# The last layer's down projection of a two-layer decoder trunk, written as seven block products instead of eight

## The chip, the cores and the metric

The kernel runs on one core of a Trainium2 chip, as one program and one launch. The metric is device time in microseconds (us). The core has five engines that work side by side, each through its own stream of instructions in a fixed order: TensorE (PE in the profile; its weight loads are PEld), VectorE (DVE), ScalarE (ACT), GpSimd (POOL) and SyncE (SP), which here only issues DMAs. Where an instruction needs another engine's result it waits for a semaphore, and everything behind it in its own stream waits too.

## The reference

Two layers, each a token mixer with three branches and then a gated MLP with a short causal convolution, and a final RMSNorm. There are 512 tokens of width 1024, in float32. Only the end of the second layer is touched by the change:

```python
def conv_ffn(h, w_up, conv_w, conv_b, w_down):
    u = h @ w_up
    ...
    gate, val = jnp.split(c, 2, axis=-1)
    return (jax.nn.silu(gate) * val) @ w_down

x = x + conv_ffn(rmsnorm(x, norm2_g[l]), ffn_w_up[l], ffn_conv_w[l], ffn_conv_b[l], ffn_w_down[l])
...
return rmsnorm(x, final_g)
```

The product with w_down has 512 rows (tokens), an inner dimension of 2816 (22 blocks of 128) and 1024 columns. The activation silu(gate) * val comes out with the inner dimension on the partitions, 128x512 for each of the 22 blocks.

## The kernel before

Matrices are multiplied in float32 by splitting each operand into a rounded high part and the rest. ACT casts the high part (line 135 for weights, 1066 for activations), DVE subtracts it from the original for the low part (136, 1067), and `mm3` (line 152) issues three matmuls: high x low, high x high, low x high. A matmul has a 128x128 block as its stationary operand and 128x512 as its moving one.

`ffn_up` runs the up projection for i = 0 to 21. For each i it makes two columns of blocks (gate and value), scales them (1054), convolves (1056 to 1058), applies the gate (1062 to 1064) and splits the result into the pair `act[i]`. For odd i under 17 it also turns one block of the residual x into rows, over DRAM with POOL's DMA queue (`turned`, 226 and 230), into `xt`.

`last` is the down projection of the second layer and the end of the program. The stationary operand is a block of an activation (128 tokens), the moving one a weight tile (128x512). First all four row blocks c of the left half of the columns: for k in 22, one weight unit and 4 x 3 matmuls into four PSUM tiles of the pool `acc`. Then the right half, into four PSUM tiles of the pool `sm`: 16 units in the same way, and the last 6 (`KEPT`) are kept in memory, so that row blocks finish one after another and the scaling and output of a row block run beside the products of the next. The left half's sums are read from PSUM, added to x (1106), squared (1109) and multiplied by the final gain on POOL (1123) while the right half is multiplied. The row's scale comes from a root on ACT (1137) and a reciprocal on DVE (1138); ACT scales the left half (1149), DVE the right one (1151), and ACT's and SP's queues write them out.

Weight units are loaded by SP and split a few units ahead (`unit`, `load`, `part`). The order of instructions on each engine is set when the program is built, by a scheduler that works from the program's order with its own estimates; instructions under `keep_in_program_order` (`po`, and every matmul while `self.pin` is set) stay as written.

Of the kernel before, what the change touches and what calls it, by code (L numbers as in the profile page):

```python
# [48 lines left out]
class Emit:  # L49
# [95 lines left out]
        self.nc.vector.tensor_tensor(lo, src, hi, op=SUB)  # L145
        return hi, lo

    def mm3(self, ps, w, x, start, stop):
        (wh, wl), (xh, xl) = w, x

        def mm(*x, **y):
            i = self.nc.tensor.matmul(*x, **y)  # L152
# [881 lines left out]
    def ffn_up(self, l, st, x):  # L1034
        nc, V, A = self.nc, self.nc.vector, self.nc.scalar
        nt = [0]
        self.xt = []

        def at():
            nt[0] += 1  # L1040
            return (self.f if nt[0] <= NFP else self.r)(dt=F32R, n="ah")

        act = []
        first = self.firstF(l, (78, 79, 80), st, (3,))
        for i in range(NFF):
            if x and i % 2 == 1 and i < 17:
                o = self.r(n="xt")
                self.turned(o, self.r(n="xT"), x[i // 2], nc.gpsimd)
                self.xt.append(o.rearrange("p (a c d) -> p c a d", c=4, d=32))
            cs = []  # L1050
            for j in (i, NFF + i):
                ps = first.pop(0) if first else self.colF(l, 78 + 2 * i + (j >= NFF))
                u = self.u(n="fu")
                V.tensor_tensor(u, ps, self.rsF, op=MUL)  # L1054
                t = self.u(n="cv")
                A.activation(t, u, AF.Identity, scale=self.p("cw2", j), bias=self.p("cb", j))  # L1056
# [7 lines left out]
            V.tensor_tensor(th, th, v, op=MUL)  # L1064
# [22 lines left out]
    def last(self, act):  # L1087


        nc, V, A, P, po = self.nc, self.nc.vector, self.nc.scalar, self.nc.gpsimd, self.tc.keep_in_program_order  # L1090
        fg = [self.u(n="fg") for _ in range(2)]
        for h in range(2):
            nc.sync.dma_start(fg[h], self.a["fgr"][:, 512 * h:512 * h + 512].to_broadcast([128, 512]))
        ss, bias = self.small((128, NC), "fss", 1), self.small((128, NC), "fbi", 1)
        self.pin = True

        def prod(ps, k, c, w):
            cs = slice(128 * c, 128 * c + 128)
            ah, al = act[k]
            self.mm3(ps, (ah[:, cs], al[:, cs]), w, k == 0, k == NFF - 1)  # L1100

        def add(y, ps, j, c):

            b = slice(j % 4 * 128, j % 4 * 128 + 128)
            q = lambda t: t[:, b].rearrange("p (a d) -> p a d", d=32)
            return V.scalar_tensor_tensor(q(y), q(ps), 0.5, self.xt[j][:, c], op0=MUL, op1=ADD)

        def square(y, s):
            return A.activation(self.u(n="sq")[:, 0:y.shape[1]], y, AF.Square, accum_out=s)

        self.pool = None
        pss = [self.acc() for _ in range(NC)]
        for k in range(NFF):
            w = self.unit("wdt", 0, k, 0)
            for c in range(NC):
                prod(pss[c], k, c, w)
        ya = []
        for c in range(NC):
            y = self.u(n="ya")
            for j in range(4):  # L1120
                add(y, pss[c], j, c)
            square(y, ss[:, c:c + 1])
            P.tensor_tensor(y, y, fg[0], op=MUL)
            ya.append(y)
        V.tensor_scalar(bias, ss, 1.0 / D, 1e-6, op0=MUL, op1=ADD)
        pss = [self.sm() for _ in range(NC)]
        for k in range(NFF - KEPT):
            w = self.unit("wdt", 0, k, 512)
            for c in range(NC):
                prod(pss[c], k, c, w)  # L1130
        self.pool = "u"
        ws = [self.unit("wdt", 0, k, 512) for k in range(NFF - KEPT, NFF)]

        def factor(s, b):

# [2 lines left out]
            po(V.reciprocal(rs, rs))  # L1138
            return rs

        for c in range(NC - 1):
            for k, w in enumerate(ws, NFF - KEPT):
                prod(pss[c], k, c, w)
            y, s = self.u(n="yb"), self.small((128, 1), "fs1")
            for j in range(4, 8):
                po(add(y, pss[c], j, c))
            po(square(y, s))
            rs = factor(s, bias[:, c:c + 1])
            po(A.activation(ya[c], ya[c], AF.Copy, scale=rs))
            nc.scalar.dma_start(self.a["out"][c, :, 0:512], ya[c])  # L1150
            po(V.scalar_tensor_tensor(y, y, rs, fg[1], op0=MUL, op1=MUL))
            nc.sync.dma_start(self.a["out"][c, :, 512:1024], y)
        c, y, b = NC - 1, self.u(n="yb"), bias[:, NC - 1:]
        for k, w in enumerate(ws, NFF - KEPT):
            prod(pss[c], k, c, w)
        for j in range(4, 8):
            po(add(y, pss[c], j, c))
        s = [self.small((128, 1), f"fs{i}", 1) for i in (2, 3)]
        for i in range(2):
            po(square(y[:, 256 * i:256 * i + 256], s[i]))  # L1160
        po(V.scalar_tensor_tensor(b, s[0], 1.0 / D, b, op0=MUL, op1=ADD))
        rs = factor(s[1], b)
        for i in range(2):
            h = slice(256 * i, 256 * i + 256)
            po(V.scalar_tensor_tensor(y[:, h], y[:, h], rs, fg[1][:, h], op0=MUL, op1=MUL))
            nc.sync.dma_start(self.a["out"][c, :, 512 + 256 * i:768 + 256 * i], y[:, h])
            po(A.activation(ya[c][:, h], ya[c][:, h], AF.Copy, scale=rs))
            nc.scalar.dma_start(self.a["out"][c, :, 256 * i:256 * i + 256], ya[c][:, h])

# [111 lines left out]
```

## Time and profile before

| | |
|---|---|
| Time of three runs | 1712.87, 1715.34, 1715.23; median 1715.23 us |
| Span of the profiled execution | 1712.1 us |
| Down projection of the last layer, left half | 1585.8 to 1645.7 us |
| Right half | 1645.8 to 1705.65 us |
| Rest after the last matmul | 1705.65 to 1712.1 us |

The profiled execution is another one than the three timed; its own time is the span from the first instruction to the last. Rows of instruction groups give line, engine, operation, output and inputs by the program's names, shapes, the count, and the busy time with the mean of one in ns; then the engine's idle time before them and who ended it. Rows of a timeline give start and duration in us. Rows of a tile's view give the shortest, median and longest duration in ns, and the first and last start in us. Rows of windows give the stretch, its length, busy time and count of PE, PEld, DVE, ACT and POOL, the granted clock of TensorE, the share of DMA and GB/s.

### The profile page before, as it was taken

The page shows a single profiled execution, that of the slowest core. Times are in us where ns is not written, and L with a number is a line of the kernel's source. Part 1 is how long each engine was busy: PE and PEld are TensorE (multiplying, and loading weights), DVE is VectorE, ACT ScalarE, POOL GpSimd, SP SyncE. Part 2 cuts the span into 40 slices and gives each one's busy share as a digit, 9 for nine tenths or more (in the row PEclk, how much of TensorE's full clock was granted, in tenths as well). Part 3 has the DMA queues.
Part 4 walks back from the last instruction along what each step waited for, and adds up shares of the span by engine and source line. Part 5 has one row for each costly group of instructions (what it writes and reads, how often), then busy time and mean ns, then how long its engine had stood idle before and what let it go on. Part 6 is the DMA issues. An engine that isn't in the chain of part 4 may idle for free.

```text
span 1712.1 us, 27377 instructions
## 1 busy us (share of the span) xinstructions
PE 1701.0 (99%) x10280; PEld 1392.4 (81%) x10280; DVE 1155.0 (67%) x1998; ACT 774.9 (45%) x1315; POOL 178.2 (10%) x213
## 2 busy tenths in 40 slices
PE   9999999999999999999999999999999999999998
PEld 7888777788888888888888888777888888888886
DVE  6887745578669777753368887555776787787333
ACT  6563443554255444433355634345533554444223
POOL 2121000003200000000021210100141011100010
PEclk9999999999999999999999999999999999999999
DMA  5236553525542333233432365535254433333333
GB/s 180 87 109 205 174 174 99 178 89 163 163 148 93 98 99 96 69 113 114 123 105 87 107 222 168 159 122 178 77 185 147 137 122 117 113 109 99 99 99 105
DMA packets 132325, 219.61 MB, mean 128 GB/s; under 512 B 16864, under 2 KB 37088, under 8 KB 132192
## 3 DMA queue, kind: packets, MB, share of 16 engines
q1 hardware_dynamic: 116336, 180.94, 34.4%
q0 software_dynamic: 6784, 20.98, 3.8%
q10 hardware_dynamic: 9072, 15.94, 2.6%
q8 instruction: 81, 1.33, 0.3%
q14 instruction: 52, 0.43, 0.1%
HBM read 188.43 MB, written 29.36 MB: 127 GB/s over the span
## 4 chain that ended last, share of the span: by engine, by line
PE 89%; DMA 5%; DVE 3%; ACT 1%; issue 1%; SPq 1%; ACTq 0%; POOL 0%; DVEq 0%; POOLq 0%
PE acc L152 80%; PE sm L152 4%; PE sm L640 2%; DMA wr<-wall 2%; PE sm L893 1%; DVE wl L136 1%; PE sm L547 1%; DMA ws<-sgw 1%; DMA tr<-yt 0%; DMA tr<-bkT 0%; SPq L226 0%; DMA bkS<-tr 0%; PE sm L998 0%; DMA x<-xT 0%; DMA tr<-qkt 0%
## 5 line engine op out<-in xcount | busy, mean ns | idle before, releaser
L152 PE MATMUL acc<-hi,sh 128*128 128x512 f32 x1108 | 431.9, 390 | 0.0
L152 PE MATMUL acc<-lo,sh 128*128 128x512 f32 x1108 | 431.6, 390 | 0.0
L152 PE MATMUL acc<-hi,sl 128*128 128x512 f32 x1108 | 430.6, 390 | 0.0
L135 ACT CAST sh<-wr 128x512 fp32r<-128x512 f32 (+1 forms) x347 | 212.2, 615 | 356.6 <-PE acc L152 264.3
L136 DVE TENSOR_TENSOR sl<-wr,sh 128x512 fp32r<-128x512 f32 (+1 forms) x347 | 236.1, 683 | 139.9 <-ACT sh L135 74.9
L136 DVE TENSOR_TENSOR wl<-wr,wh 128x512 fp32r<-128x512 f32 x233 | 165.2, 710 | 184.9 <-ACT wh L135 182.3
L135 ACT CAST wh<-wr 128x512 fp32r<-128x512 f32 x233 | 144.1, 619 | 281.1 <-PE acc L152 182.3
L152 PEld LDWEIGHTS acc<-hi,sl 128*128 128x128 f32 x1108 | 208.0, 188 | 43.7 <-DVE gth L1013 0.3
L152 PEld LDWEIGHTS acc<-lo,sh 128*128 128x128 f32 x1108 | 208.0, 188 | 43.6 <-issue 0.9
L152 PEld LDWEIGHTS acc<-hi,sh 128*128 128x128 f32 x1108 | 208.0, 188 | 43.6 <-issue 0.3
L152 PE MATMUL acc<-lo,wh 128*128 128x512 f32 x588 | 232.5, 395 | 0.5 <-DVE lo L211 0.3
L152 PE MATMUL acc<-hi,wl 128*128 128x512 f32 x588 | 230.3, 392 | 0.5 <-DVE wl L136 0.5
L152 PE MATMUL acc<-hi,wh 128*128 128x512 f32 x588 | 229.5, 390 | 0.0
L152 PEld LDWEIGHTS acc<-lo,wh 128*128 128x128 f32 x588 | 110.5, 188 | 26.3 <-DVE lo L211 1.6
L152 PEld LDWEIGHTS acc<-hi,wl 128*128 128x128 f32 x588 | 110.5, 188 | 25.9 <-DVE wl L136 2.3
L152 PEld LDWEIGHTS acc<-hi,wh 128*128 128x128 f32 x588 | 110.6, 188 | 22.4 <-issue 0.2
L152 PE MATMUL acc<-ah,sh 128*128 128x512 f32 x352 | 108.4, 389 | 0.0
L1054 DVE TENSOR_TENSOR fu<-acc,rsF 128x512 f32<-128x512 f32 x88 | 60.6, 688 | 56.4 <-PE acc L152 56.3
L1056 ACT ACTIVATE cv<-fu,pc 128x512 f32<-128x512 f32 x88 | 71.6, 816 | 46.7 <-DVE fu L1054 44.4
L1057 DVE SCALAR_TENSOR_TENSOR cv<-fu,pc,cv 128x511 f32<-128x511 f32 x88 | 65.8, 748 | 21.1 <-ACT cv L1056 20.6
L152 PE MATMUL acc<-wl,hi 128*128 128x512 f32 x192 | 78.3, 408 | 0.0
L152 PEld LDWEIGHTS acc<-ah,sh 128*128 128x128 f32 x352 | 66.1, 188 | 13.7
(312 smaller groups left out, 2345.4 us busy)
## 6 DMA issues: line engine op xcount, KB each, us to landing
wr<-wall SPq DMA_DIRECT2D x488, 256.0 KB, 2.7
gd<-gth ACTq DMA_DIRECT2D x48, 256.0 KB, 3.0
gth<-gd POOLq DMA_DIRECT2D x48, 256.0 KB, 3.6
wr<-wdt SPq DMA_DIRECT2D x44, 256.0 KB, 2.6
wr<-wdn SPq DMA_DIRECT2D x40, 256.0 KB, 2.7
tr<-bkT SPq DMA_DIRECT2D x16, 256.0 KB, 2.8
bkS<-tr SPq DMA_DIRECT2D x128, 32.0 KB, 2.5
tr<-vT SPq DMA_DIRECT2D x8, 256.0 KB, 2.6
```

Of the source, the lines that this page charges most:

```text
L135: self.kept(self.nc.scalar.copy(hi[:, :n], raw[:, :n]))
L136: self.kept(self.nc.vector.tensor_tensor(lo[:, :n], raw[:, :n], hi[:, :n], op=SUB))
L152: i = self.nc.tensor.matmul(*x, **y)
L547: i = T.matmul(pK[hv[1 - h], j, :], bk[hv[h], c, 1, :], x[hv[h], c, :], start=True, stop=True)
L640: po(T.matmul(o, l, r, start=start, stop=True, skip_group_check=True))
L893: po(T.matmul(X[h][:, i, :], lhsT, rhs, start=new[h], stop=stop, skip_group_check=True))
L1054: V.tensor_tensor(u, ps, self.rsF, op=MUL)
L1056: A.activation(t, u, AF.Identity, scale=self.p("cw2", j), bias=self.p("cb", j))
L1057: V.scalar_tensor_tensor(t[:, 1:], u[:, :511], self.p("cw1", j), t[:, 1:], op0=MUL, op1=ADD)
```

## The change

The product is divided into 2 x 2 x 2 blocks: rows (tokens 0 to 255, 256 to 511), inner dimension (even and odd blocks of 128, so a pair q = 0 to 10 is blocks 2q and 2q+1) and columns (left, right). Instead of eight block products, seven are made, with sums of halved blocks on both sides. They are numbered 1 to 7 in the code. Products 7, 5, 6 and 4 use sums of weight blocks; products 1, 2 and 3 use weight blocks as they are. Products 1, 2 and 4, 3 use activations as they are or one sum of all four.

In `ffn_up` of the last layer, `halves` takes the two activations a and b of a pair and makes, on POOL, s (two sums of 256 tokens), d and the difference that replaces the left of b; s and b are split for group 1. The unsummed halves (`ab`) and d (two pairs to a tile, `s4`) go to DRAM by POOL's DMA queue.

In `last`, group 1 runs over q: `sums(q)` loads four weight blocks and makes four sums of them, three on POOL and one on DVE; `ring` splits each of them (ACT and DVE). `sums(q + 1)` is written ahead of the products of q. After a pair's products its `ab` tile is loaded again and split. Group 2 runs product 1 over all q, then 3 and 2 over the first six pairs, then 2 and 3 over the five kept ones row block by row block. The four PSUM results of a row block are combined into v1, v2 and v3 between the groups, and x is added on POOL (`addx`, four pieces of 128 columns). Rows 2 and 3 are finished after product 1; rows 0 and 1 at the end. `KEPT` goes from 6 to 5.

```diff
-KEPT = 6
+KEPT = 5
...
-    def mm3(self, ps, w, x, start, stop):
+    def mm3(self, ps, w, x, start, stop, **kw):
...
-            hi, lo = at(), at()
-            A.copy(hi, th)
-            V.tensor_tensor(lo, th, hi, op=SUB)
-            act.append((hi, lo))
+            if l < L - 1:
+                act.append(self.split(th, at))
+            elif i % 2 == 0:
+                even = th
+            else:
+                act.append(self.halves(even, th, i // 2, at))
         return act
+
+    def halves(self, a, b, q, at):
+        P, h = self.nc.gpsimd, [slice(0, 256), slice(256, 512)]
+        s, d = [self.wp.tile([128, 512], F32, name=self.nm(t), tag=t, bufs=3) for t in ("wh", "wl")]
+        P.tensor_tensor(s[:, h[0]], a[:, h[1]], b[:, h[1]], op=ADD)
+        P.tensor_tensor(s[:, h[1]], s[:, h[0]], a[:, h[0]], op=SUB)
+        P.tensor_tensor(d[:, h[0]], b[:, h[0]], s[:, h[1]], op=SUB)
+        ab = self.dp.tile([128, 512], F32, name=self.nm("ab"))
+        if q % 2 == 0:
+            self.s4 = self.dp.tile([128, 512], F32, name=self.nm("s4"))
+        for o, i in ((ab[:, h[0]], a[:, h[0]]), (ab[:, h[1]], b[:, h[0]]), (self.s4[:, h[q % 2]], d[:, h[0]])):
+            P.dma_start(o, i)
+        P.tensor_tensor(b[:, h[0]], a[:, h[0]], a[:, h[1]], op=SUB)
+        return self.split(s, at), self.split(b, at), ab, self.s4
...
+        Q, H = NFF // 2, [slice(0, 512), slice(512, 1024)]
+        def ring(w):
+            nring[0] += 1
+            if nring[0] % 2:
+                hi, lo = [self.wp.tile([128, 512], F32R, name=self.nm(t), tag=t, bufs=3) for t in ("wh", "wl")]
+            else:
+                hi, lo = [self.u(dt=F32R, n=t) for t in ("sh", "sl")]
+            A.copy(hi, w)
+            V.tensor_tensor(lo, w, hi, op=SUB)
+            return hi, lo
...
+        def sums(q):
+            b12, b22, b11, b21 = [raw(2 * q + j, n) for j, n in ((0, 1), (1, 1), (0, 0), (1, 0))]
+            P.tensor_tensor(b22, b22, b12, op=SUB)
+            P.tensor_tensor(b12, b12, b11, op=SUB)
+            V.tensor_tensor(b11, b11, b22, op=ADD)
+            P.tensor_tensor(b21, b21, b11, op=SUB)
+            return [ring(w) for w in (b22, b12, b11, b21)]
...
+        pss = {p: [(self.acc if p in (7, 5) else self.sm)() for _ in range(2)] for p in (7, 5, 6, 4)}
+        W, ab = [sums(0)], []
...
+        for q in range(Q):
+            if q + 1 < Q:
+                W.append(sums(q + 1))
+            s, t = act[q][:2]
+            w = dict(zip((7, 5, 6, 4), W.pop(0)))
+            for p in (7, 5, 6, 4) if q < Q - 1 else (6, 7, 5, 4):
+                x, at = {7: (t, 0), 5: (s, 0), 6: (s, 256), 4: (t, 256)}[p]
+                for r in range(2):
+                    prod(pss[p][r], x, at, r, w[p], q == 0, q == Q - 1)
+            o = self.u(n="ab")
+            nc.sync.dma_start(o, act[q][2])
+            ab.append(self.split(o, self.f))
...
+        seq = [(1, q) for q in range(Q)]
+        k0 = Q - KEPT
+        for g in range(0, k0, 3):
+            seq += [(p, q) for p in (3, 2) for q in range(g, min(g + 3, k0))]
+        kept = [(p, q) for p in (2, 3) for q in range(k0, Q)]
...
+        def addx(y, h, c):
+            for j in range(4):
+                b = y[:, 128 * j:128 * j + 128].rearrange("p (a d) -> p a d", d=32)
+                P.tensor_tensor(b, b, self.xt[4 * h + j][:, c], op=ADD)
+        def plus(y, ps, z, rows=slice(0, 512)):
+            return V.scalar_tensor_tensor(y[:, rows], ps[:, rows], 0.5, z[:, rows], op0=MUL, op1=ADD)
...
+        ahead(3)
+        for r in range(2):
+            e, f, g = [self.f(n=t) for t in ("v1", "v2", "v3")]
+            A.activation(e, pss[6][r], AF.Copy, scale=0.5)
+            plus(f, pss[7][r], e)
+            plus(g, pss[5][r], e)
+            plus(e, pss[4][r], f)
+            plus(f, pss[5][r], f)
+            addx(e, 0, 2 + r)
+            addx(f, 1, 2 + r)
+            addx(g, 1, r)
...
+        for p, q in seq:
+            ahead(1)
+            for r in range(2):
+                go(p, q, r, units[p, q])
+            if (p, q) != (1, Q - 1):
+                continue
+            for r in range(2):
+                plus(v3[r], one[r], v3[r])
+                plus(v1[r], one[r], v1[r])
+                plus(v2[r], one[r], v2[r])
+            for r in range(2):
+                c, (ya, yb) = 2 + r, (v1[r], v2[r])
+                s1, b = self.small((128, 1), "fs1"), ss[:, c:c + 1]
+                square(ya, b)
+                square(yb, s1)
+                V.tensor_scalar(b, b, 1.0 / D, 1e-6, op0=MUL, op1=ADD)
+                rs = self.small((128, 1), "frs", 4)
+                A.activation(rs, s1, AF.Sqrt, scale=1.0 / D, bias=b)
+                V.reciprocal(rs, rs)
+                P.tensor_tensor(ya, ya, fg[0], op=MUL)
+                A.activation(ya, ya, AF.Copy, scale=rs)
+                nc.gpsimd.dma_start(self.a["out"][c, :, 0:512], ya)
+                V.scalar_tensor_tensor(yb, yb, rs, fg[1], op0=MUL, op1=MUL)
+                nc.gpsimd.dma_start(self.a["out"][c, :, 512:1024], yb)
...
+        ahead(len(kept))
+        for r in range(2):
+            for p, q in kept:
+                go(p, q, r, units[p, q])
...
```

`ahead(n)` loads and splits the next n weight tiles of group 2 (through `ring`, or into kept tiles), `go` issues the three matmuls of one weight tile and one block of 128 rows, and `raw` is a load of one 128x512 weight tile by SP.

More of the change, by code (lines that the diff above doesn't have):

```diff
@@ L1037, in ffn_up, with at @@
         self.xt = []
-        def at():
+        def at(**kw):
             nt[0] += 1
@@ new lines, in last, with ahead @@
+        kept = [(p, q) for p in (2, 3) for q in range(k0, Q)]
+        units, todo = {}, iter(seq + kept)
+        def ahead(n):
+            for _, (p, q) in zip(range(n), todo):
+                w = raw(2 * q + (p > 1), p == 3)
+                if (p, q) in kept:
+                    hi, lo = [self.u(dt=F32R, n=t) for t in ("sh", "sl")]
+                    A.copy(hi, w)
+                    V.tensor_tensor(lo, w, hi, op=SUB)
+                    units[p, q] = hi, lo
+                else:
+                    units[p, q] = ring(w)
@@ L1125, in last @@
[L1125 to L1132, printed above, removed]
         def factor(s, b):
@@ L1139, in factor @@
             return rs
[L1141 to L1168, printed above, removed]
+        ahead(3)
@@ new lines, in last @@
+        v1, v2, v3 = [], [], []
+        for r in range(2):
[8 more added lines that the diff above has]
+            addx(g, 1, r)
+            v1.append(e), v2.append(f), v3.append(g)
+        one = [self.sm() for _ in range(2)]
@@ new lines, in last @@
+        out = {1: one, 2: one, 3: [self.acc() for _ in range(2)]}
+        for p, q in seq:
[22 more added lines that the diff above has]
+                nc.gpsimd.dma_start(self.a["out"][c, :, 512:1024], yb)
```

82 lines of the change are left out of this document (56 added, 26 removed).

## The prediction, made before the run

> **What bounds the kernel now.** I read the page's busy times and chain first, then the down projection of the last layer by its tiles, then its two stretches.
>
> ```profile
> span 1712.1 us, 27377 instructions
> PE 1701.0 (99%) x10280; PEld 1392.4 (81%) x10280; DVE 1155.0 (67%) x1998; ACT 774.9 (45%) x1315; POOL 178.2 (10%) x213
> PE 89%; DMA 5%; DVE 3%; ACT 1%; issue 1%; SPq 1%; ACTq 0%; POOL 0%; DVEq 0%; POOLq 0%
> ...
> L152 PE MATMUL acc<-wh,ah x176: 389/389/389, 1586.0 to 1645.4; 128*128 128x512 f32 x176
> ...
> L152 PE MATMUL sm<-wh,ah x128: 389/389/389, 1645.9 to 1688.9; 128*128 128x512 f32 x128
> ...
> L152 PE MATMUL acc<-wl,ah x88: 389/389/389, 1585.8 to 1645.0; 128*128 128x512 f32 x88
> ...
> L152 PE MATMUL sm<-wl,ah x64: 389/389/389, 1645.6 to 1688.5; 128*128 128x512 f32 x64
> ...
> L152 PE MATMUL sm<-sh,ah x48: 388/389/389, 1689.4 to 1705.3; 128*128 128x512 f32 x48
> ...
> L152 PE MATMUL sm<-sl,ah x24: 389/389/389, 1689.2 to 1704.8; 128*128 128x512 f32 x24
> ...
> 1645.80 59.85 PE sm L152 x264
> 1705.65 0.02 issue
> ...
> 1585.60:1645.40 59.80, 59.80 (x265) 49.53 (x264) 19.27 (x32) 15.13 (x25) 0.00 (x0) 1.00 0.30 96
> 1645.40:1705.70 60.30, 60.24 (x266) 49.55 (x264) 23.89 (x52) 21.36 (x41) 5.95 (x4) 1.00 0.31 98
> ```
>
> TensorE is the bound of the whole program and more so here: 176 + 128 + 88 + 64 + 48 + 24 = 528 matmuls run from 1585.8 to 1705.65 without a break. A record lasts 389 ns but matmuls overlap; the chain row gives the price on the path, 59.85 / 264 = 0.2267 us. In the same two stretches DVE is busy for 43 of 120 us, ACT for 36, POOL for 6, and DMA 0.3 of its capacity. All those helpers are hidden behind TensorE; after the last matmul there are 6.45 us of row scaling and output.
>
> **What is removed.** Seven products of eight leave 7 x 11 x 2 x 3 = 462 matmuls: 66 x 0.2267 = **-15.0 us**, the whole possible gain, if TensorE still never waits. The rest of this part asks where it waits.
>
> **Group 1 and the lock between DVE and POOL.** Per pair q of inner blocks, TensorE has 4 products x 2 x 3 = 24 matmuls, 5.44 us. The new helpers for one q: POOL subtracts three times 128x512, DVE adds once and splits five times (four weight sums, one reloaded ab tile), ACT casts five times, SP loads five tiles of 256 KB. Counted apart they fit, with durations from the rows here and below: POOL 3 x 1.29 = 3.9, DVE 6 x 0.68 = 4.1, ACT 5 x 0.62 = 3.1; DMA moves 1.31 MB, 241 GB/s, by the row above (0.31 at 98) a share of 0.76. But the only POOL tensor operations in the old down projection show that they cannot be counted apart:
>
> ```profile
> 1646.13 1.29 POOL L1123 TENSOR_TENSOR ya<-ya,fg 128x512 f32<-128x512 f32 x1 [132.26 <-ACT sq L1109]
> 1646.79 1.18 DVE L136 TENSOR_TENSOR wl<-wr,wh 128x512 fp32r<-128x512 f32 x1
> 1647.38 1.74 POOL L1123 TENSOR_TENSOR ya<-ya,fg 128x512 f32<-128x512 f32 x1
> ...
> 1649.08 1.29 POOL L1123 TENSOR_TENSOR ya<-ya,fg 128x512 f32<-128x512 f32 x1
> ...
> 1649.26 1.66 DVE L136 TENSOR_TENSOR wl<-wr,wh 128x512 fp32r<-128x512 f32 x1 [0.50 <-ACT wh L135]
> ...
> 1650.33 1.74 POOL L1123 TENSOR_TENSOR ya<-ya,fg 128x512 f32<-128x512 f32 x1
> 1652.01 0.68 DVE L136 TENSOR_TENSOR wl<-wr,wh 128x512 fp32r<-128x512 f32 x1
> ```
>
> A DVE split that meets no POOL operation takes 0.68 (last row). The two that start inside one end 0.55 after it: 1647.97 against 1647.42, and 1650.92 against 1650.37. The POOL operations that start inside such a split end 1.15 after it: 1649.12 and 1652.07. They take turns, whole instruction by whole instruction, with 1.15 for POOL and 0.55 for DVE. So one q needs 3 x 1.15 + 6 x 0.55 = 6.75 us of turns, more than TensorE's 5.44, and group 1 is bound by the turns: 11 x 6.75 - 11 x 5.44 = **+14.4 us**. Below: no waiting for turns, where POOL's own loop (two subtractions, DVE's add, the third: 2 x 1.25 + 0.1 + 0.69 + 1.29 = 4.6) stays under 5.44, so 0. Above: turns of full length, 3 x 1.29 + 6 x 0.68 = 7.95, so 11 x 2.51 = 27.6. I take the measured turns.
>
> [...]
>
> **Start of group 1.** Before, k = 0 needs only old activations, so TensorE goes straight on while the last one is finished:
>
> ```profile
> 1585.57 0.39 PE L152 MATMUL acc<-hi,sl 128*128 128x512 f32 x1
> 1585.80 0.39 PE L152 MATMUL acc<-wl,ah 128*128 128x512 f32 x1
> ...
> 1586.00 0.69 DVE L1054 TENSOR_TENSOR fu<-acc,rsF 128x512 f32<-128x512 f32 x1 [1.22 <-PE acc L152]
> ...
> 1589.51 0.68 DVE L136 TENSOR_TENSOR wl<-wr,wh 128x512 fp32r<-128x512 f32 x1
> 1590.11 0.68 DVE L1064 TENSOR_TENSOR fth<-fth,cv 128x512 f32<-128x512 f32 x1
> ...
> L226 POOL DMA_DIRECT2D xt<-tr x32 | 17.4, 551 | 20.1 <-PE acc L152 9.2 <-ACT sh L135 6.0 <-ACT cv L1056 2.6
> ```
>
> In the changed program's order, POOL's stream has the first subtraction of sums(0), then the first operation of halves for the last pair, then a DMA issue, and only then the second subtraction of sums(0). That halves operation waits for the last activation, which ends at 1590.79, 4.8 us after the last up-projection matmul (4.2 without the weight split that then stood between). Behind it: POOL 0.75 (128x256, half of 1.29 and some start; bounds 0.65, and 0.96 with the 0.31 of POOL's smallest copy, below) + 0.55 + 1.29 = 2.6. DVE's stream then has the add, the split of b12 and only third the split of b22, which the first product reads: 3 x 0.6 alone (DVE starts back to back stand 0.6 apart: 1589.51, 1590.11), or with turns against two halves operations and the third subtraction 4.2. Sum 4.5 + 2.6 + 4.2 = **+11.3**, bounds 8.6 and 12.7. No other matmul stands between, so nothing covers it.
>
> **Up projection.** halves adds to each pair four 128x256 POOL operations and three POOL DMAs. ACT's stream has both casts of a pair's sums ahead of weight casts; for the last pair but one five weight casts stand directly behind. From the activation, POOL's chain to the second sum is 4 x 0.75 + 2 x 0.55 + waits, some 4.8 us. Weights are cast some microseconds ahead; I charge half, **+2.4** (0 to 5). Earlier pairs are taken as covered.
>
> **The rows finished in the middle.** After the products with p = 1, rows 2 and 3 are finished, and ACT's stream holds the whole of it, both rows, ahead of the weight cast for the product (2, 0). TensorE has 18 matmuls of (3, 0..2) for cover, 4.1 us.
>
> ```profile
> L135 ACT CAST wh<-wr 128x512 fp32r<-128x512 f32 x38 | 23.7, 623 | 67.5 <-PE acc L152 40.5 <-PE sm L152 21.8 <-DMA wr<-wdt 2.9
> ...
> L1137 ACT ACT_TABLE_LOAD x1 | 1.3, 1283 | 0.0
> ...
> L1109 ACT ACTIVATE sq<-ya 128x512 f32<-128x512 f32 x4 | 2.5, 626 | 1.6 <-DVE ya L1106 1.6
> ...
> L1151 DVE SCALAR_TENSOR_TENSOR yb<-yb,frs,fg 128x512 f32<-128x512 f32 x3 | 2.3, 752 | 0.1
> ...
> L1149 ACT ACTIVATE ya<-ya,frs 128x512 f32<-128x512 f32 x3 | 2.2, 725 | 0.9 <-DVE frs L1138 0.9
> ...
> L1137 ACT ACTIVATE frs<-fs,fbi 128x1 f32<-128x1 f32 x4 | 1.2, 294 | 0.1
> ...
> L1109 ACT ACTIVATION_READ_ACCUMULATOR sq<-ya 128x1 f32 x4 | 0.7, 185 | 0.0
> L1138 DVE RECIPROCAL frs<-frs 128x1 f32<-128x1 f32 x4 | 0.7, 164 | 5.2 <-ACT frs L1137 5.2
> ...
> L271 POOL COPY rs<-rst 32x4 f32<-32x4 f32 x4 | 1.3, 314 | 14.4 <-DVE rst L268 14.2
> ```
>
> First row of the two: three DVE reads of PSUM 2.0, square 0.8, then the bias step on DVE behind two weight splits that meet POOL's product with fg 1.3, table load 1.3, root and reciprocal 0.6: 6.0. DVE's stream puts the second row's reads behind that reciprocal: 0.7; POOL adds four 128x128 pieces of x, issues the first row's two output DMAs, adds four more: 8 x 0.48 + 1.1 = 4.9 (a quarter of 1.29 is 0.32, with the 0.31 of a POOL copy of almost nothing 0.64; I take the middle). Then a DVE read 0.75, square 0.8, root and reciprocal 0.6, scaling 0.73, the cast 0.62, the split 0.68: 4.2. In all 15.8, less 4.1: **+11.7**. Bounds: the pieces give 1.3 either way, uncontended splits 1 less: 9.4 to 13.
>
> **Small ones.** At the joint of the groups the ab weights' splits share DVE with the reads of PSUM, and the last row's read is 512 wide instead of four pieces: **+1.5** (0 to 3).
>
> **The clock.** TensorE has no idle time in the old stretch, so a long stall is new. The nearest row is the program's start:
>
> ```profile
> 1.52 4.63 PE L310 MATMUL acc<-rst 128*128 128x256 f32 x10 [1.52 <-DVE rst L307]
> ...
> 6.90 0.63 PE L152 MATMUL acc<-hi,wl 128*128 128x512 f32 x1
> 7.33 0.56 PE L152 MATMUL acc<-lo,wh 128*128 128x512 f32 x1
> 7.73 0.39 PE L152 MATMUL acc<-hi,wh 128*128 128x512 f32 x1
> 7.96 0.40 PE L152 MATMUL acc<-hi,wl 128*128 128x512 f32 x1
> ```
>
> Matmuls stand 0.42 apart until 7.7 and 0.23 after: about half rate for up to 6 us after work begins. If a stall brings it back, the first one's is hidden under the turns, the middle one's is not: half of 3 to 6 us. I take **+1.5** (0 to 3).
>
> [...]
>
> **Sum.** -15.0 + 14.4 + 11.3 + 2.4 + 11.7 + 1.5 + 1.5 = +27.8. Against the execution's own span: 1739.9; the median of the runs, 1715.23, lies 3.1 above that span, so 1743.0.
>
> **Rivals.**
> 1. TensorE keeps the bound: the separate counts (3.9, 4.1, 3.1 under 5.44) speak for it, the turns against. It decides if both long stalls and group 1 together cost under 15; a queue order in which POOL's second subtraction and ACT's weight cast are not stuck would do it. Then -15.0 + 2.4 + 1.5 = -11.1: 1704. Chance 0.05. Its mechanism needs three waits to be absent that the instruction order shows.
> 2. No turns: POOL and DVE overlap in group 1, only the stalls remain at their lower ends: -15.0 + 8.6 + 2.4 + 9.4 + 1.5 = +6.9: 1722. For it: few rows carry the turns. Against: every overlap in them shows it. Chance 0.10, of which 0.02 lands within the bound of no change and 0.01 below.
> 3. Half rate through group 1: with gaps in each q the slow clock might stay. 24 matmuls at 0.42 are 10.1 us per q against 6.75: 11 x 3.35 = 37 more, 1780. Only the start rows show a half rate here. [...] Chance 0.05.
> 4. The change doing something else: the changed stream has 66 TensorE rows fewer, as it should; no chance kept.
>
> The forecast has 0.80. Its own range is 1732 to 1757, the terms' bounds taken together at about two thirds. With rival 2 the range is **1724 to 1757**. About 0.2% is what can be told from no change: faster 0.06, same 0.02, slower 0.92.
>
> **What would show it.** TensorE's first gap over 8 us right before the first product of group 1, ended by a DVE split; in group 1 gaps in every q, DVE splits of 1.2 us and more beside POOL operations of 1.7, and 74 us for its 264 matmuls; a gap near 10 us before (2, 0) ended by a split behind ACT's scaling of row 3. I am wrong if group 1 takes 60 us, if either long gap is under 4, or if the matmuls after a gap stand 0.42 apart for more than 6 us.

## The result, and the profile after

The changed kernel takes 1758.93 us (median of four runs, 1757.48 to 1760.74) against 1715.28 (four runs, 1712.87 to 1718.77): a ratio of 1.0258, 95% interval 1.0242 to 1.0273. It is slower by 43.7 us where 27.8 were forecast, and 1.9 us over the end of the range. The profiled execution has a span of 1755.8 us, 43.7 more than that of before.

The page of the changed kernel begins:

```profile
span 1755.8 us, 27707 instructions
PE 1712.2 (98%) x10214; PEld 1383.2 (79%) x10214; DVE 1244.0 (71%) x2054; ACT 802.5 (46%) x1367; POOL 301.1 (17%) x351
```

TensorE has 66 instructions fewer, and yet 11.2 us more of busy time. So idle gaps are only a part of the loss: matmuls themselves have become slower somewhere.

The windows of the stretch that the change rewrites: the gap ahead of it, group 1, group 2, and the end.

```profile
1598.80:1609.80 11.00, 0.21 (x1) 0.00 (x0) 7.21 (x8) 3.96 (x7) 6.26 (x7) 0.63 0.71 249
1609.80:1689.70 79.90, 71.56 (x266) 51.94 (x267) 76.93 (x78) 38.48 (x67) 51.24 (x35) 0.92 0.59 188
1689.70:1749.00 59.30, 48.77 (x198) 37.93 (x196) 34.33 (x62) 24.05 (x48) 20.79 (x30) 0.91 0.38 123
1749.00:1755.80 6.80, 0.00 (x0) 0.00 (x0) 1.87 (x5) 2.22 (x7) 0.00 (x0) 0.70 0.22 77
```

In group 1, DVE is busy for 76.9 of 79.9 us, where TensorE's 264 matmuls would need 59.85. TensorE stood still for the 11 us ahead of it, and its granted clock is below 1 in each of the windows (0.63, 0.92, 0.91 and 0.70), where it is 1.00 in both stretches of before.

**The start of group 1.** The timeline of the changed kernel, TensorE, then POOL, then DVE:

```profile
1598.62 0.39 PE L152 MATMUL acc<-hi,sl 128*128 128x512 f32 x1
1610.04 0.79 PE L152 MATMUL acc<-wl,ah 128*128 128x512 f32 x1 [11.04 <-DVE wl L1121]
1610.63 1.05 PE L152 MATMUL acc<-wh,ah 128*128 128x512 f32 x2
...
1595.08 1.30 POOL L1132 TENSOR_TENSOR raw<-raw,raw 128x512 f32<-128x512 f32 x1
1603.44 0.72 POOL L1077 TENSOR_TENSOR wh<-fth,fth 128x256 f32<-128x256 f32 x1 [7.06 <-DVE fth L1064]
1604.10 0.56 POOL L1084 DMA_DIRECT2D ab<-fth  x1
1604.68 1.27 POOL L1133 TENSOR_TENSOR raw<-raw,raw 128x512 f32<-128x512 f32 x1
...
1605.99 1.20 DVE L1134 TENSOR_TENSOR raw<-raw,raw 128x512 f32<-128x512 f32 x1 [2.63 <-POOL raw L1133]
1607.11 1.21 DVE L1121 TENSOR_TENSOR sl<-raw,sh 128x512 fp32r<-128x512 f32 x1
1608.24 1.74 DVE L1121 TENSOR_TENSOR wl<-raw,wh 128x512 fp32r<-128x512 f32 x1
```

This is read as an order: the first subtraction is done at 1596.4, and then POOL idles for 7.06 us in front of a halves operation that waits for the last activation. The second subtraction stands behind it and a DMA issue; then come the add and two splits at a slowed pace (1.20, 1.21 and 1.74 us, where 0.68 is the time beside an idle POOL), of which the second is the one that the first product reads. From 1598.62 to 1610.04 are 11.42 us; less a normal step of 0.23, 11.2 us are lost. Behind it the matmuls are slow: the first step, 1610.04 to 1610.63, is 0.59, and ten of the next eleven are 0.427.

**The rows finished in the middle.** DVE, then ACT, then TensorE of the changed kernel:

```profile
1704.37 1.89 DVE L1196 SCALAR_TENSOR_TENSOR v<-sm,v 128x512 f32<-128x512 f32 x3 [5.74 <-PE sm L152]
...
1708.54 0.67 DVE L1196 SCALAR_TENSOR_TENSOR v<-acc,v 128x512 f32<-128x512 f32 x1
...
1716.07 0.69 DVE L1196 SCALAR_TENSOR_TENSOR v<-sm,v 128x512 f32<-128x512 f32 x1 [1.12 <-POOL v L1193]
...
1718.13 0.72 ACT L1243 ACTIVATE v<-v,frs 128x512 f32<-128x512 f32 x1 [0.29 <-DVE frs L1241]
1718.76 0.60 ACT L1120 CAST wh<-raw 128x512 fp32r<-128x512 f32 x1
...
1720.14 0.80 PE L152 MATMUL sm<-wl,hi 128*128 128x512 f32 x1 [9.88 <-DVE wl L1121]
```

From the first PSUM read at 1704.37 to TensorE's start at 1720.14 pass 15.8 us, and the weight cast stands behind the scaling of the second row. A row to note is 1708.54: a read of `acc`, thus of a result of group 1 for row 3, in the midst of finishing row 2.

### The profile page after: what moved, and what is told of

It is laid out like the page before. It is cut to its first block, busy times and chain, and to the rows that moved or that the text cites. A ratio compares the mean times of both kernels' runs of the same rounds, so it can differ in the third digit from the quotient of the medians.

```text
span 1755.8 us, 27707 instructions
## 1 busy us (share of the span) xinstructions
PE 1712.2 (98%) x10214; PEld 1383.2 (79%) x10214; DVE 1244.0 (71%) x2054; ACT 802.5 (46%) x1367; POOL 301.1 (17%) x351
## 5 line engine op out<-in xcount | busy, mean ns | idle before, releaser
L135 ACT CAST sh<-wr 128x512 fp32r<-128x512 f32 (+1 forms) x341 | 208.2, 616 | 359.1 <-PE acc L152 257.6
L136 DVE TENSOR_TENSOR wl<-wr,wh 128x512 fp32r<-128x512 f32 x195 | 137.5, 706 | 126.2 <-ACT wh L135 122.9
L135 ACT CAST wh<-wr 128x512 fp32r<-128x512 f32 x195 | 120.3, 618 | 213.6 <-PE acc L152 144.0
L1057 DVE SCALAR_TENSOR_TENSOR cv<-fu,pc,cv 128x511 f32<-128x511 f32 x88 | 70.4, 801 | 23.1 <-ACT cv L1056 22.9
L152 PEld LDWEIGHTS acc<-ah,sh 128*128 128x128 f32 x352 | 66.1, 188 | 15.8
```

The source lines that it names most:

```text
L135: self.kept(self.nc.scalar.copy(hi[:, :n], raw[:, :n]))
L136: self.kept(self.nc.vector.tensor_tensor(lo[:, :n], raw[:, :n], hi[:, :n], op=SUB))
L152: i = self.nc.tensor.matmul(*x, **y, **kw)
```

## The experiments

Each is compared with the kernel before, run on the same chip beside it. "Aligned" is the base for most of them.

### Matmuls slowed before any changed instruction

The last matmul of the up projection starts at 1598.62, against 1585.57 in the profile of before: 13.05 us are lost by then, and the only new gap there is one of 2 us. The windows from 440 to 500 us, in layer 0, where no instruction was changed; first of the kernel before:

```profile
440.00:500.00 60.00, 60.00 (x266) 49.48 (x265) 37.74 (x58) 23.27 (x40) 6.96 (x9) 1.00 0.46 147
```

and of the changed kernel, with a second window from the first layer's up projection:

```profile
440.00:500.00 60.00, 60.00 (x259) 48.28 (x258) 37.69 (x58) 23.81 (x40) 6.97 (x9) 1.00 0.46 149
600.00:660.00 60.00, 60.00 (x267) 49.67 (x266) 46.29 (x72) 28.41 (x44) 0.00 (x0) 1.00 0.31 97
```

TensorE is busy all the time in all three, at a granted clock of 1.00: 60/266 = 0.226 us a matmul before, 60/259 = 0.232 after, 0.225 in the other window of after. The diff drops one small tile, `fbi`, in a line that is not printed above; it takes 32 bytes per partition in memory, and the pool ff, allocated behind it, moves by as much against the pools ahead of it. (ff holds most of the activations `ah` of the down projection, among others.) The first run keeps that tile without using it. Four others move ff in the kernel before, whose instructions stay as they are, and one moves nearly everything there.

```diff
 aligned (changed kernel):
-        ss = self.small((128, NC), "fss", 1)
+        ss, _ = self.small((128, NC), "fss", 1), self.small((128, NC), "fbi", 1)
 shift32, shift64, shift128, shift256 (kernel before; n = NC, 16, 32, 64):
-        ss, bias = self.small((128, NC), "fss", 1), self.small((128, NC), "fbi", 1)
+        ss, bias, _ = ..., self.small((128, n), "pad", 1)
 all64 (kernel before; moves every pool but the constants):
         self.con = self.cp.tile([128, NCC], F32, name="con")
+        self.cp.tile([128, 16], F32, name="pad")
```

> The changed kernel, with the small tile fbi (128x4, 32 bytes on each partition) still allocated, so that the pool of 39 tiles starts at 146752 again, a multiple of 64 bytes, and not at 146720. Layout theory: a matmul that reads a tile of that pool takes 0.2333 us apart only because the tile starts at an odd multiple of 32 bytes; all steps are 0.2267 again, the 10.6 us that the changed kernel lost before the last up projection are gone, and some 200 matmuls after group 1 save 1.3 more: 1759 - 12 = 1747. Group 1, bound by the turns of DVE and POOL, keeps its 6.9 us per q. Rival, the granted clock (0.99 in all runs of the changed kernel): the tile changes nothing, 1759.

> The kernel before with one more small tile of 32 bytes that nothing uses, so that the pool starts at 146784, an odd multiple of 32. Layout theory: the same 10.6 us appear before the last up projection, and 528 matmuls of the down projection take 0.0067 more, 3.5 us: 1715.3 + 14 = 1729. Rival, that the loss came with the change's instructions or with the clock: 1715.

> The kernel before with one more small tile of 64 bytes, the pool at 146816, a multiple of 64. Layout theory: alignment decides and not the address, so no change, 1715. If any shift of the pool costs, 1729.

> The kernel before with one small tile of 128 bytes per partition that nothing uses, ahead of the pool ff; ff's base moves by 128 bytes, no instruction changes. If what counts is where the pool lies against a grid of 128 bytes, ff stands on it as in the kernel before and the time is that of the kernel before, 1715 to 1717 us, with matmuls 0.227 us apart throughout. If any move of ff away from its old place costs, or if the pad itself does, the time is 1722 or more, as with the pad of 64 bytes.

> The kernel before with an unused tile of 64 bytes at the front of memory, so that every pool but the constants moves by 64 bytes, ff with them; their places against each other stay. If the distance of ff from the other pools decides, the time is that of the kernel before, 1715 to 1717 us. If each tile's own place against a grid of 128 bytes decides, it is at least the 1722 us of the run in which ff alone moved by 64 bytes, and more where other operands now pay too.

> The kernel before with an unused tile of 256 bytes ahead of ff, so that ff is 768 instead of 512 bytes past the other pools against a grid of 2048. If distances that are multiples of 256 are free, the time is that of the kernel before, 1715 to 1717. If the place found by chance in the kernel before is a special one, it is slower again by 6 to 14 us, 1722 to 1730, like the moves by 32, 64 and 128.

| run | ff moved against the pools ahead of it | matmuls from 440 to 500 us | median us | ratio to before, 95% |
|---|---|---|---|---|
| aligned (changed kernel) | back in place | 266 | 1748.91 | 1.0187 [1.0172, 1.0202] |
| shift32 | +32 bytes | 258 | 1729.73 | 1.0081 [1.0064, 1.0097] |
| shift64 | +64 | 264 | 1722.27 | 1.0035 [1.0022, 1.0048] |
| shift128 | +128 | 259 | 1728.68 | 1.0069 [1.0054, 1.0084] |
| shift256 | +256 | 265 | 1715.66 | 1.0004 [0.9995, 1.0013] |
| all64 | 0 (all by 64) | 265 | 1715.76 | 0.9996 [0.9986, 1.0006] |

The window of shift128, and then that of shift256, whose programs differ in nothing but the size of an unused tile:

```profile
440.00:500.00 60.00, 60.00 (x259) 48.26 (x258) 36.04 (x56) 22.66 (x39) 6.98 (x9) 1.00 0.45 144
```

```profile
440.00:500.00 60.00, 60.00 (x265) 49.48 (x264) 37.67 (x58) 23.16 (x40) 6.97 (x9) 1.00 0.46 146
```

So the place of ff costs some 10 us of the changed kernel's time, without a wait anywhere: the two medians differ by 10.0 (1758.93 - 1748.91), and each against its own runs of the kernel before by 10.9 (43.65 - 32.79). My own idea of it was wrong twice: neither a grid of 64 bytes (shift64 missed by 7 us) nor one of 128 (shift128 missed by 12) is the rule. all64 beside shift64 (1715.76 against 1722.27, with ff at the same place in both) shows that the distance between the pools counts here and not the absolute place, and of the moves of ff tried only 256 bytes was free (1.0004 [0.9995, 1.0013]). What the distance does to a matmul was not taken apart; that stays open.

### The turns between DVE and POOL

All four sums of a pair on DVE, in the aligned version:

```diff
-            P.tensor_tensor(b22, b22, b12, op=SUB)
-            P.tensor_tensor(b12, b12, b11, op=SUB)
+            V.tensor_tensor(b22, b22, b12, op=SUB)
+            V.tensor_tensor(b12, b12, b11, op=SUB)
             V.tensor_tensor(b11, b11, b22, op=ADD)
-            P.tensor_tensor(b21, b21, b11, op=SUB)
+            V.tensor_tensor(b21, b21, b11, op=SUB)
```

> As aligned, with all four sums of sums on DVE and none on POOL. Turns theory: group 1 no longer shares the turns, DVE has 9 operations of 0.6 for each q, 5.4 us, and TensorE's 5.44 is the bound: gaps of the 1.0 and 0.2 kind are gone, 11 x 1.4 = 15 us less than aligned, 1732. Rival, that the loads (five tiles of 256 KB per q, landing 3.4 us instead of 2.6) bound group 1: 6.9 us per q stay, 1747. Rival, that DVE then is the bound by more than its sum: between, 1740.

It took 1734.91 us, ratio 1.0112 [1.0097, 1.0127]: 14.0 less than aligned. A window over five pairs of group 1, from the first matmul of one pair to that of the fifth after it, first in the changed kernel and then in aligned:

```profile
1636.79:1671.34 34.55, 31.13 (x121) 21.35 (x121) 33.05 (x31) 15.02 (x25) 24.73 (x15) 1.00 0.64 211
1629.59:1664.11 34.52, 31.12 (x121) 21.37 (x121) 33.02 (x31) 15.03 (x25) 24.70 (x15) 1.00 0.65 210
```

and over five pairs in the version with the sums on DVE:

```profile
1620.06:1647.26 27.20, 27.20 (x122) 22.52 (x120) 26.49 (x43) 13.62 (x23) 0.00 (x0) 1.00 0.76 245
```

A pair takes 34.52/5 = 6.90 us with POOL and 27.20/5 = 5.44 without, TensorE's own time. DVE has more operations there (43 records against 31) in less busy time (26.5 against 33.0 us). What bound group 1 here was thus the turns, not the amount of work. In the changed kernel itself DVE's records show it as the old rows did: 0.68 us where no POOL operation is under way at its start, 1.5 to 1.8 where one is.

```profile
1644.16 0.68 DVE L1121 TENSOR_TENSOR sl<-raw,sh 128x512 fp32r<-128x512 f32 x1
1645.00 1.54 DVE L1121 TENSOR_TENSOR wl<-raw,wh 128x512 fp32r<-128x512 f32 x1 [0.16 <-ACT wh L1120]
...
1648.18 1.77 DVE L145 TENSOR_TENSOR lo<-ab,hi 128x512 fp32r<-128x512 f32 x1
```

### The gap at the start, taken away

`sums(0)` is issued in `ffn_up`, ahead of the last activation, in aligned (early) and in the version with the sums on DVE (early_dve).

```diff
 ffn_up, last layer, in the loop over i:
+            if x and i == 21:
+                self.nring = 0
+                self.w0 = self.sums(0)
 last:
-        W, ab = [sums(0)], []
+        W, ab = [self.w0], []
 ...
```

> The version with ff back at its base (1748.9 us), and the loads and sums of pair 0 of group 1 issued in the up projection, before the last pair's halves, in place of behind them. If the start of group 1 is a cost of its own beside the turns, as the prediction adds them up, the gap of 11.4 us and the slow matmuls behind it go and nothing comes in their place: about 14 us less, 1735. If the sums of pair 1, which now stand where those of pair 0 stood, are late instead, because POOL and DVE set the pace from there on, most of the gap comes back in group 1: about 2 us less, 1747.

> As the run before, with all four sums of a pair on DVE, against the version with the sums on DVE alone (1734.9 us). TensorE set the pace in that one's group 1, so here nothing is to take the place of the gap at the start: 11 us of gap and 2 to 3 of slow matmuls less, 1721. If the sums of pair 1 are late here too, the gap stays in part: 1727 or more.

They took 1745.47 us, 1.0174 [1.0159, 1.0189], and 1733.63, 1.0108 [1.0094, 1.0121]: 3.4 and 1.3 less than their bases by the medians. In both cases the intervals overlap those of the bases (1.0187 [1.0172, 1.0202] and 1.0112 [1.0097, 1.0127]), so the second gain can't be told from none. My expectation for it, 1721, was wrong. The rows of TensorE at the gap, first in early:

```profile
1606.38 0.80 PE L152 MATMUL acc<-wl,ah 128*128 128x512 f32 x1 [7.82 <-DVE wl L1083]
```

and then in early_dve:

```profile
1602.50 0.79 PE L152 MATMUL acc<-wl,ah 128*128 128x512 f32 x1 [5.52 <-DVE wl L1083]
```

Pair 0 now runs with no wait over 1.1 us, and the long gap stands before pair 1, since the sums of pair 1 are where those of pair 0 were: behind the last activation. The lateness is not removed: in early most of the gap is handed on by a pair. In early_dve about half is, 5.52 of 10.64 us, and the rest does not come back in full either: its pairs 6 to 8 take 5.71 to 5.85 us, where every such pair of its base takes 5.44. What else takes it back was not taken apart.

### The gap in the middle, by two causes

In one run (later) the finishing of rows 2 and 3 is written behind `ahead(len(kept))`, so ACT's weight casts come ahead of it. In the other (v3_r) only the tile v3 comes from another pool. Both start from aligned.

```diff
 later:
-            for r in range(2):
-                c, (ya, yb) = 2 + r, (v1[r], v2[r])
-                ...
         ahead(len(kept))
+        for r in range(2):
+            c, (ya, yb) = 2 + r, (v1[r], v2[r])
+            ...
 v3_r:
-            e, f, g = [self.f(n=t) for t in ("v1", "v2", "v3")]
+            e, f, g = self.f(n="v1"), self.f(n="v2"), self.r(n="v3")
```

> The version with ff back at its base (1748.9 us), and the finishing of rows 2 and 3 written behind the loads and casts of the last ten weight tiles, so that ACT's stream has the weight casts for (2, 0) and after ahead of the squares, roots and scalings. If the wait in the middle is ACT's order, as the prediction has it, the gap of some 10 us before (2, 0) goes with its slow matmuls, 10 to 12 us less: 1737 to 1739. If it is that the reads of PSUM of row 3 come late because its tile v3 gets no free buffer, the products that need those PSUM tiles still wait: about 4 us less, 1745.

> The version with ff back at its base (1748.9 us), and v3 of the two rows taken from the pool r instead of ff; nothing else. If the gap in the middle comes from v3 of the second row waiting for a free buffer of ff, it shrinks from some 10 us to about 2 to 5 and its slow matmuls go: 8 to 9 us less, about 1740. If the gap is ACT's order alone, nothing changes: 1749.

They took 1743.54 us, 1.0155 [1.0140, 1.0170], and 1743.88, 1.0155 [1.0140, 1.0170], about 5 less than aligned each. Neither theory alone is enough. In later, DVE and TensorE where the gap ends:

```profile
1705.14 0.69 DVE L1196 SCALAR_TENSOR_TENSOR v<-sm,v 128x512 f32<-128x512 f32 x1 [0.75 <-POOL v L1193]
...
1705.89 0.80 PE L152 MATMUL sm<-wl,hi 128*128 128x512 f32 x1 [5.14 <-DVE v L1196]
```

In v3_r, DVE, ACT and TensorE there:

```profile
1698.12 3.68 DVE L1196 SCALAR_TENSOR_TENSOR v<-sm,v 128x512 f32<-128x512 f32 x6 [3.29 <-PE sm L152]
...
1706.13 1.40 DVE L1245 SCALAR_TENSOR_TENSOR v<-v,frs,fg 128x512 f32<-128x512 f32 x2
1707.44 0.69 DVE L1121 TENSOR_TENSOR wl<-raw,wh 128x512 fp32r<-128x512 f32 x1
...
1704.24 1.28 ACT L1240 ACT_TABLE_LOAD   x1 [1.66 <-DVE fss L1238]
1705.92 0.60 ACT L1120 CAST wh<-raw 128x512 fp32r<-128x512 f32 x1
...
1702.46 0.50 PE L152 MATMUL acc<-wl,hi 128*128 128x512 f32 x1 [2.40 <-DVE wl L1121]
1708.18 0.72 PE L152 MATMUL sm<-wl,hi 128*128 128x512 f32 x1 [2.37 <-DVE wl L1121]
```

With the casts out of the way, the gap is 5.14 us and ends with a read of PSUM: product 2 writes the tile that holds product 1, and the last read of it, for row 3, waits for POOL to add x to a tile that was made late. With v3 in another pool, POOL's adds are done by 1697.7, before product 1 ends, and the six reads run in one go. Two waits of 2.4 us are left there: in the first a weight split stands on DVE behind the six reads, in the second the cast stands on ACT behind the roots and its split on DVE behind the scaling of the rows. So two waits ran side by side in the changed kernel, and each hid what the other cost.

### All of it together, and on to the limit of DVE

combined has aligned's tile, the sums on DVE, sums(0) early, v3 from the other pool and the finishing behind the casts, with the PSUM reads kept in program order. two issues the sums of pairs 0 and 1 early; two_last also has the last pair's products in the order of the others.

```diff
 two, against combined:
-            if x and i == 21:
-                self.nring = 0
-                self.w0 = self.sums(0)
+            if x and i in (19, 21):
+                self.nring = self.nring if i == 21 else 0
+                self.w0 = (self.w0 if i == 21 else []) + [self.sums(i // 2 - 9)]
 ...
 two_last, against two:
-            for p in (7, 5, 6, 4) if q < Q - 1 else (6, 7, 5, 4):
+            for p in (7, 5, 6, 4):
```

> ff back at its base, all four sums on DVE, the sums of pair 0 in the up projection, v3 from the pool r, the finishing of rows 2 and 3 behind the last weight casts. By the gaps that the single runs measured (11 at the start, 10 in the middle, 2 to 3 of slow matmuls after each, 14 of turns) what is left of the loss against before is the up projection's 2, the joint's 4 and some at the end, against the 15 of the removed matmuls: 1708 to 1712. If the helpers' work only moves from one gap to the next, about 1717, that of the kernel before. It does not reach 1700, which would be all of the removed matmuls' time.

> The combined version (1718.9 us) with the sums of pairs 0 and 1 both issued in the up projection, at the activations 19 and 21. If the gap of 5.7 us before pair 1 stands because its sums queue on DVE behind the last activation, it goes with its slow matmuls (2.7): about 1711. If DVE's work around the last activation is too much in all, the gap moves to pair 2, or the up projection itself waits more: 1716 to 1720.

> The run before, with the products of the last pair in the order of all others (7, 5, 6, 4). If the gap of 2.7 us at the last pair (3.7 in the changed kernel) comes from its product 6 being first while its weight sum is split third, the gap goes with its slow matmuls: 3 to 4 us less than two. If it is the joint of the groups, the PSUM reads are now later and a gap at the first product of group 2 takes its place: the same time as two or up to 3 more.

| run | median us | ratio to before, 95% |
|---|---|---|
| combined | 1718.88 | 1.0024 [1.0014, 1.0034] |
| two | 1720.37 | 1.0020 [1.0010, 1.0029] |
| two_last | 1719.68 | 1.0022 [1.0013, 1.0031] |

combined is 3.5 us over before (1718.88 - 1715.36), aligned 32.8 (1748.91 - 1716.12): 29.3 are won back, and the middle of it is clean: the window of group 2 in combined, 198 matmuls in 45 us, is all TensorE.

```profile
1667.00:1712.00 45.00, 44.77 (x198) 36.73 (x196) 34.04 (x64) 24.41 (x50) 21.06 (x32) 1.00 0.47 152
```

None of the three beats the kernel before. combined was to take 1708 to 1712 if the gains of the single runs added up; they do not, and it keeps a gap of 5.50 us before pair 1 and one of 2.52 before the last pair. What two shows is why: the gap before pair 1 is down to 0.87 us, but the one in the up projection grew from 2 to 6.37, and five pairs of group 1 take 29.25 us.

```profile
1582.89 0.80 PE L152 MATMUL acc<-lo,sh 128*128 128x512 f32 x1 [6.37 <-ACT sh L135]
1609.90 0.50 PE L152 MATMUL acc<-wl,ah 128*128 128x512 f32 x1 [0.87 <-DVE wl L1083]
...
1622.77:1652.02 29.25, 28.71 (x121) 22.13 (x121) 28.44 (x46) 15.04 (x25) 0.00 (x0) 1.00 0.68 229
```

That is 5.85 us a pair with DVE busy for 28.4 of 29.25. The 5.44 of the version with the sums on DVE came with a start 11 us late, which DVE had used to work ahead; without that lead DVE's nine operations a pair (four sums, five splits) set the pace. In combined the lead is seen to run out: its pairs 2 to 5 take 5.44 us, the next 5.49 and the two behind it 5.85. In two_last the last pair's gap is gone, and one of 2.70 stands before the first product of group 2, as the second theory had it:

```profile
1663.89 0.47 PE L152 MATMUL sm<-wl,hi 128*128 128x512 f32 x1 [2.70 <-ACT wh L1082]
```

## Why the prediction was wrong

The direction and the long mechanisms held. The sum lacked a term; the clock and the small ones were too small, the pace of group 1 too large. The measured column is from the profiled execution of the changed kernel, the working of each entry beside it.

| term | predicted | measured | from |
|---|---|---|---|
| 66 matmuls fewer | -15.0 | -15.0 | 10280 to 10214 instructions |
| up projection | +2.4 | +2.1 | one gap, at 1584.8 |
| start of group 1 | +11.3 | +11.2 | step of 11.43 |
| pace of group 1 | +14.4 | +9.5 | pairs 2 to 8: 47.6 against 7 x 5.44 |
| joint, last pair, last row | +1.5 | +5.5 | 4.4 at the last pair (1.5 of it is the pace of a pair), 0.7 at 1706.9, 0.4 at the end |
| rows finished in the middle | +11.7 | +10.0 | step of 10.26 |
| clock | +1.5 | +7.5 | 30 steps of 0.427 and three of 0.28 to 0.40 in three places (6.4), and the step ahead of each (1.1) |
| place of ff in memory | none | +12.9 | 13.05 less 2.1 before group 1; some 2 is what is left of the 43.7 |

The last entry closes the sum at 43.7; its first part is measured, its second is the remainder. The first part is good to some 2 us: shift256 and all64, which cost nothing, are 2.0 and 1.7 us behind the profile of before at the same matmul. aligned, which puts ff back, is 10.0 us faster by the medians.

**The step that failed** is the one that makes the sum "against its own span", with everything ahead of the changed instructions taken as it was, and each matmul at 0.2267 us wherever helpers keep up. It read the diff as a list of instructions. The line that drops `fbi` removes no work at all, but it moves ff, and matmuls that no other line of the diff touches grew from 0.226 to 0.232. aligned is the prediction's own case, the change without that move: 32.8 us over before by the medians, against 27.8 forecast, and 1748.9 lies inside the range. That it comes so near is in part luck: the pace was forecast 4.9 us too high, and the last pair and the joint 4.0 too low.

**The clock** was named and under-sized: half rate was charged once, for the middle. It came three times, since the last pair had a long gap too, and the first was not "hidden under the turns". The first two pairs are not bound by turns: the sums of pair 0 are made during the wait and those of pair 1 during the slow products of pair 0, and pair 1 took 5.60 us. The three stretches of half rate (the granted clock reads 0.50) each begin in the gap and last beyond it:

```profile
1601.60:1615.20 13.60, 5.16 (x12) 4.09 (x13) 10.93 (x10) 4.28 (x8) 10.01 (x10) 0.50 0.51 175
1680.10:1686.90 6.80, 5.77 (x14) 4.57 (x15) 6.66 (x11) 6.34 (x13) 0.43 (x1) 0.50 0.50 152
1714.30:1724.40 10.10, 4.26 (x10) 3.39 (x11) 6.11 (x12) 6.45 (x14) 4.06 (x8) 0.50 0.38 131
```

From TensorE's start the half rate lasts 5.2, 5.8 and 4.3 us; the prediction's bound, 6 us after a gap, held. That a stall brings the half rate back was the author's assumption, and no run shows the 1.5 us as such: the rows of before that the prediction prints have steps of 0.42 us at the program's start alone. In its place the changed kernel showed steps of 0.427 us behind each of its three long gaps, which with the steps beside them come to 7.5 us.

**The pace** was right in size, 6.90 against 6.75 a pair, and wrong in how often: seven pairs and not eleven, since the first two are not bound, the last but one is counted with the gap behind it, and beside the last pair's products no sums are left to make. That the turns are the cause is what the version with the sums on DVE shows.

**The last pair** was not seen. Its products run in another order, 6 first, while the weight sums are split in the old one, so its first product waits for the third split. Its gap was 3.7 us. two_last, with the sums on DVE, shows that it moves to the joint when the order is put back.

**The start** came out to 0.1 us, and part by part: 4.4 us to POOL's halves operation, 2.5 to the end of the second subtraction and 4.1 to the split, against 4.5, 2.6 and 4.2. But it was not a cost of its own that could be added or removed: early gave back 3.4 us of it by the medians. The term's upper bound, 12.7, does not come out of the parts that it names (4.8 + 2.8 + 4.2 = 11.8), nor is the lower end of the forecast's own range, 1732, two thirds of the terms' lower bounds; neither moves the range of 1724 to 1757.

**The middle** held by the order it described, though its single chain was two waits. Rival 1 needed the two long gaps and the pace of group 1 to cost under 15 us together; they cost 11.2 + 10.0 + 9.5. Rival 2 (no turns) and rival 3 (half rate through group 1) fall by the windows: 6.90 us a pair, and a granted clock of 1.00 in the five-pair windows, where waits of 0.6 to 0.8 us recur in every pair.

## What to carry to other kernels

An edit that only adds or drops a small tile moves what is allocated behind it, and here 32 bytes took the matmul's step from 0.226 to 0.232 us: before explaining a difference, count matmuls per window in a stretch that the edit did not touch, and give the tile back if the count has changed. DVE and POOL took turns here, and a pair was priced by the turns (6.90 us), not by the two busy times that were counted apart (DVE 4.1, POOL 3.9); moving the work to DVE was the cheaper choice (5.44) even though DVE then did more. When helpers are near the bound, as here, a gap that is removed in one place can be asked for again by the next step: of the 10.64 us before pair 0 with the sums on DVE, 5.52 stood before pair 1 in early_dve. What decided was the helper's time per step (5.85 us on DVE against TensorE's 5.44), so by these runs the saving on TensorE needs helpers that stay below it.

## What the runs showed of the hardware that was not expected

**The distance between pools in memory.** With the instructions of before and a granted clock of 1.00, the average step of the matmuls in the window from 440 to 500 us went from 0.226 to 0.233 and 0.232 us when one pool, ff, moved by 32 or 128 bytes against the others (258 and 259 matmuls for 266); a move by 64 cost less (264 matmuls, and 6 us in all), and one by 256, or of all pools together, nothing (265 matmuls each, ratios of 1.0004 and 0.9996). In that window of the changed kernel a matmul's record lasts 395 to 396 ns in the median, in place of 389.

**Half rate after a gap of 2 us.** The same gap in the up projection, 1.94 or 1.95 us long in the profiles of eight of the kernels, was followed by slow matmuls in three of them (aligned, later, v3_r) and not in the other five: the longest record of the up projection's matmuls from 1570 us on is 628 to 770 ns in the three and 500 to 504 in the five. In the changed kernel:

```profile
1584.83 0.50 PE L152 MATMUL acc<-lo,sh 128*128 128x512 f32 x1 [1.95 <-ACT sh L135]
1585.16 0.40 PE L152 MATMUL acc<-hi,sh 128*128 128x512 f32 x1
```

and in aligned, with the window behind the gap:

```profile
1576.36 0.77 PE L152 MATMUL acc<-lo,sh 128*128 128x512 f32 x1 [1.95 <-ACT sh L135]
1576.92 0.63 PE L152 MATMUL acc<-hi,sh 128*128 128x512 f32 x1
...
1576.40:1579.80 3.40, 3.40 (x8) 2.75 (x9) 2.29 (x4) 0.94 (x2) 0.00 (x0) 0.50 0.35 101
```

By the trace's clock records, the stretches of half rate last 13.65, 6.83 and 10.24 us in the three places of the changed kernel, 4, 2 and 3 times 3.41; in aligned the window above reads 0.50 for 3.40.

In the changed kernel's gaps of 11.04, 3.52 and 9.88 us the granted clock fell at 1601.6, 1680.1 and 1714.2, which is 2.6, 2.5 and 4.0 us after the end of TensorE's last record. In aligned it was 0.50 from the end of a gap of 1.95 us on, and in the changed kernel it was 1.00 through a gap of the same length and behind it. So neither the length of a gap nor one fixed delay accounts for what was measured; what in a gap decides between half and full rate stays open.
